# Hybrid retention/MLA step: the sample rows' latents in plain float32 on four column groups, with the first loads reordered

## The chip, the cores and the metric

The kernel runs on one core of a Trainium2 chip. The metric is the device time of one execution in microseconds (us). Before the change the median of 3 runs is 2147.01 us (2147.0 to 2148.47). Verdicts compare medians of runs on the same chip.

## The reference

One layer of a hybrid decoder is computed for 1024 prompt rows and 32 sample rows (8 sequences of 4 tokens), model width 1024. What matters here is its start: the normalised input times one wide matrix, of which the "latent" columns (384 + 256 + 64 = 704) are normalised again and rotated.

```
z = rmsnorm(x, ln_w) @ w_in
rq, rk, rv, rg, cq, ckv, kr, mg, ga, gb = jnp.split(z, ...)
q = (rmsnorm(cq, q_norm_w) @ w_uq).reshape(b, s, MLA_HEADS, MLA_QK)
ckv = rmsnorm(ckv, kv_norm_w)
kr = rope(kr, pos)
```

Behind it come paged attention of the sample rows over 8192 past tokens each, retention, prompt attention, and the output projections. The gates (`rg`, `mg`, `ga`, `gb`) are further columns of `z`.

## The kernel before

All large products take float32 operands split into a high part (rounded to float32r) and a low part (the rest); `mac` issues three matmuls for each product of two such pairs (lines 265 to 267). The high part of a weight is a cast on ACT or POOL, the low part a subtraction on DVE (`lo_of`, L199).

**First stage, the latents.** The 1056 rows are nine tiles: 0 to 7 are the prompt's 128 rows each, tile 8 the 32 sample rows. The order is 0, 1, 8, 2, 3, 4, 5, 6, 7. For each tile:

- `load_x` brings the rows in (L302; four rooms `xt`).
- `turn_tile` squares and sums the rows on ACT (L347, into `xs`), makes the reciprocal root on POOL (`rs_v`, `rs_r`), transposes the tile on PE in eight 128x128 pieces (L322), copies them out of PSUM (L323, `turn`), and stores them (`xTD`).
- `scale_tile` spreads the reciprocal root over the columns with one small matmul on PE (L355), multiplies on DVE (`y`, L358), and makes the high part on ACT (`xh`, L363) and the low part on DVE (`xl`, L364).
- `latent_tile` runs 2 x 8 x 3 = 48 matmuls (columns 0 to 383, then 384 to 703) into PSUM tiles `ac`, of which there are three, then normalises (ACT L398, POOL `rs`, DVE L400), rotates (DVE L374 to L379), stores `la` (two rooms; `latS` for the sample rows) and stores a blockwise transpose (`lt`, L330, `latD`).

The latent weight is 8 blocks of 128 x 704, loaded by `load_lat` into four rooms `wlr`; its high parts are cast alternately on ACT and POOL.

**The filler.** `gate_tiles` gives one column block of 128 gate columns after another: `load_w` loads it in two halves (L245, two rooms `wr`), POOL casts `wh`, DVE makes `wl`, and 72 matmuls follow in three thirds of 352 rows; each third is copied out by ACT (L416, `gev`) and stored (L417, `ga`). `beside` draws such work from the generator `fill` while it runs the first stage, and again beside the sample queries and the paged attention. The sample queries start with transposes of `latS` (L506) and a product of 12 float32 matmuls of 32 rows on four column groups (L527). `page_rows` loads the page table and makes the index column for the gathers; its two tiles share the rooms `xs`.

The written order is not the executed one: a scheduler places the instructions of each engine, and each engine then runs its own list strictly in order. SP issues nearly all loads and stores, also in order.

These lines are the core of the latents' product, and the product by column groups that exists already:

```
for ps, lo, w in ((pq, 0, QL), (pk, QL, KL + ROPE)):
    for k in range(8):
        xk = tuple(v[:, t * P:t * P + n] for v in xn[k])
        wk = tuple(v[:, lo:lo + w] for v in wlat[k])
        mac(ps[:n, :w], xk, wk, k == 0, k == 7)
```

```
pe.matmul(ps[c * NR:(c + 1) * NR, :384], cqT[:, k, :], wq[c][:, k], start=k == 0,
          stop=k == 2, tile_position=(0, c * NR), skip_group_check=True)
```

Of the kernel before, what the change touches and what calls it, by code (L numbers as in the profile page):

```python
# [9 lines left out]
F32 = mybir.dt.float32  # L10
F32R = mybir.dt.float32r
BF16 = mybir.dt.bfloat16
I32 = mybir.dt.int32
# [148 lines left out]
def decode_step(ctx: ExitStack, tc: tile.TileContext, A: dict, O: dict):  # L162
# [20 lines left out]
    def ac():  # L183
        return banks["pool"].tile([P, 512], F32, tag="ac", name="ac", bufs=3)
# [41 lines left out]
    def small(pl, tag, w=1, bufs=4):  # L226
        return pl.tile([P, w], F32, tag=tag, name=tag, bufs=bufs)

    def rstd_of(pl, ss, n, scale, by=pool, w=1):

        v = small(pl, f"rs_v{w}", w, 4 if w == 1 else 2)
        by.tensor_scalar(v[:n], ss[:n], scale, EPS, op0=ALU.mult, op1=ALU.add)
        r = small(pl, f"rs_r{w}", w, 4 if w == 1 else 2)
        pool.tensor_tensor(out=r[:n], in0=v[:n], in1=nhalf[:n].to_broadcast([n, w]), op=ALU.pow)
        return r
# [68 lines left out]

    def load_lat(k):
        hi, lo = (p1.tile([P, NLAT], F32R, tag=f"wl{s}{k}", name=f"wl{s}{k}", bufs=1) for s in "hl")
        raw = p1.tile([P, NLAT], F32, tag="wlr", name="wlr", bufs=4)
        sp.dma_start(raw, w_in[k * P:(k + 1) * P, C_LAT:C_LAT + NLAT])
        (hi_pool if k % 2 else act.copy)(hi, raw)
        lo_of(lo, raw, hi)  # L310
        wlat.append((hi, lo))

    def turn_input(t, src, dst, nf, by=act.copy):

        n = rows(t)
        turned = []
        for half in range(0, nf, 4):
            st = p1.tile([P, 4, P], F32, tag="turn", name="turn", bufs=4)
            w = min(4, nf - half)
            pt = tr()  # L320
            for i in range(w):
                pe.transpose(pt[:, i * P:i * P + n], src[:n, (half + i) * P:(half + i + 1) * P], ident[:n, :n])  # L322
            by(st[:, :w, :n], pt[:, :w * P].rearrange("p (a b) -> p a b", a=w)[:, :, :n])  # L323
# [18 lines left out]
    def turn_tile(t):  # L342
        n = rows(t)
        xt = xts.pop(t)
        ss = small(p1, "ss")
        xs = p1.tile([P, D], F32, tag="xs", name="xs", bufs=2)
        act.activation(xs[:n], xt[:n], AF.Square, accum_out=ss[:n])  # L347
# [35 lines left out]
    latS = lp.tile([NR, NLAT], F32, name="latS")  # L383
    idx = lp.tile([P, NB * NPG // 16], I32, name="idx")

    def latent_tile(t):
        n = rows(t)
        pq, pk = ac(), ac()
        for ps, lo, w in ((pq, 0, QL), (pk, QL, KL + ROPE)):
            for k in range(8):  # L390
                xk = tuple(v[:, t * P:t * P + n] for v in xn[k])
                wk = tuple(v[:, lo:lo + w] for v in wlat[k])
                mac(ps[:n, :w], xk, wk, k == 0, k == 7)
        la = latS if t == 8 else p1.tile([P, NLAT], F32, tag="la", name="la", bufs=2)
        cq, kv, kr = la[:n, 0:QL], la[:n, QL:QL + KL], la[:n, QL + KL:NLAT].unsqueeze(1)
        for src, dst, w, nw in ((pq[:n, :QL], cq, QL, qnw), (pk[:n, :KL], kv, KL, kvw)):
            ss = small(p1, "ss2")
            act.activation(dst, src, AF.Square, accum_out=ss[:n])  # L398
            r = rstd_of(p1, ss, n, 1.0 / w)
            dve.scalar_tensor_tensor(out=dst, in0=src, scalar=r[:n], in1=nw[:n], op0=ALU.mult, op1=ALU.mult)  # L400
        rope_nat(kr, pk[:n, KL:KL + ROPE].unsqueeze(1), t, n, p1, 1, "kro")
        if t < 8:
            sp.dma_start(O["ckv_prompt"][0, 0, t * P:(t + 1) * P, :], kv)
            sp.dma_start(O["krope_prompt"][0, 0, t * P:(t + 1) * P, :], la[:, QL + KL:])
            turn_blocks(latD, p1.tile([P, NLAT], F32, tag="lt", name="lt", bufs=2), la, t, P)
        else:
            sp.dma_start(O["ckv_sample"].rearrange("l b t c -> (l b t) c"), kv)
            sp.dma_start(O["krope_sample"].rearrange("l b t c -> (l b t) c"), la[:n, QL + KL:])

    def gate_tiles(col, dst, fs, func):  # L410
        for f in fs:
            w = load_w(w_in[:, col + f * P:col + (f + 1) * P], 8)

            def evac(j, ps, sl, f=f):
                t = wst.tile([P, TH], F32, tag="gev", name="gev", bufs=2)
                act.activation(t, ps, func)  # L416
                sp.dma_start(dst[f][:, sl], t)  # L417
            yield from gemm(w, xn, evac, 8)
# [6 lines left out]
                 gate_tiles(C_RG, [t[:, f, :] for t in gtD for f in range(4)], range(16), AF.Silu), gate_tiles(C_MG, mgD, range(4), AF.Silu))  # L425

    def page_rows():
        pt_all = p1.tile([P, NB * NPG], I32, tag="xs", name="pt_all", bufs=2)
        sp.dma_start(pt_all, A["page_table"].rearrange("b n -> (b n)").unsqueeze(0).to_broadcast([P, NB * NPG]))
        own = p1.tile([P, NB * NPG], F32, tag="xs", name="own", bufs=2)  # L430
# [5 lines left out]
        dve.tensor_scalar(idx, row, C("mod"), None, op0=ALU.add)  # L436

    head = at["maskT"][0]
# [6 lines left out]
    for k in range(8):  # L445
# [8 lines left out]
    load_x(order[3])  # L454

    def latents():
        for n, t in enumerate(order):
# [5 lines left out]
            if n == 0:  # L463
                turn_tile(order[2])
# [5 lines left out]
            if n == 4:  # L470
                page_rows()
            yield 7.1 if n > 5 else 0.0

    beside(latents(), 3 * 7.1, fill, 36)
# [1151 lines left out]
```

## Time and profile before

| what | value |
|---|---|
| median of 3 runs | 2147.01 us |
| the profiled execution, its own time | 2157.48 us |
| its span, first to last instruction | 2155.6 us |
| PE busy, of the span | 98% |
| DVE / ACT / POOL busy | 58% / 34% / 15% |
| mean granted PE clock | 0.996 |
| mean share of the 16 DMA engines, slice by slice | 0.1 to 0.7, mean 143 GB/s |

The first stage and the filler that stands among it take the first 142 us of the span; after it PE has the paged attention with filler (to about 740 us), retention (to about 1390), prompt attention (to about 1650) and the output projections.

In the timeline a row gives the start and the duration in us, the engine, the line, what is written and read, the shape, the count, and in brackets how long the engine was idle before and what ended that. PE's matmuls overlap: the distance from one start to the next is what a matmul costs, not its duration.

### The profile page before, as it was taken

What the parts mean: (1) busy time and instruction counts of PE and PEld (TensorE: products, weight loads), DVE (VectorE), ACT (ScalarE), POOL (GpSimd) and SP (SyncE); (2) the same over time, 40 slices, a digit from 0 to 9 for tenths busy, and PEclk for the clock granted to TensorE, in tenths of its full rate; (3) what the DMA queues carried; (4) which work ended last, traced back from release to release, by engine and by line L of the source; (5) the groups of instructions that cost most, each with busy time, mean ns of one, the idle gap of its engine ahead of it and who ended that gap; (6) DMA issues with size and microseconds to landing.
All of it is one profiled execution on the core that took longest, in us unless ns stands there. A gap on an engine that the chain in (4) does not pass through costs nothing. (4 is left out here: it accounts for less than half of the span.)

```text
span 2155.6 us, 38512 instructions
## 1 busy us (share of the span) xinstructions
PE 2112.4 (98%) x15192; PEld 1841.9 (85%) x15192; DVE 1260.7 (58%) x2846; ACT 724.1 (34%) x1528; POOL 326.7 (15%) x519
## 2 busy tenths in 40 slices
PE   8999999999999999999999999899999999999998
PEld 7898777777778897888888887788888999999998
DVE  5534555565655346667676774877777353444465
ACT  5412222433433222222222221454556341222243
POOL 2210111111100022222122220122221000000022
PEclk9999999999999999999999999999999999999999
DMA  7476656566565332553634628220112453324243
GB/s 209 123 223 225 238 185 231 200 245 222 186 239 176 112 85 65 162 158 103 217 72 126 198 74 265 69 53 12 38 57 81 143 178 100 95 84 126 79 143 118
DMA packets 325877, 307.84 MB, mean 143 GB/s; under 512 B 91648, under 2 KB 283264, under 8 KB 321600
## 3 DMA queue, kind: packets, MB, share of 16 engines
q1 hardware_dynamic: 316480, 221.50, 34.3%
q0 software_dynamic: 9216, 83.89, 10.3%
q8 instruction: 119, 1.95, 0.4%
q14 instruction: 62, 0.51, 0.1%
HBM read 236.96 MB, written 68.36 MB: 142 GB/s over the span
## 5 line engine op out<-in xcount | busy, mean ns | idle before, releaser
L265 PE MATMUL mm<-xh,wh 128*128 128x352 f32 x1344 | 456.6, 340 | 0.9 <-ACT gev L416 0.8
L267 PE MATMUL mm<-xh,wl 128*128 128x352 f32 x1344 | 435.2, 324 | 2.1 <-DVE wl L199 2.1
L266 PE MATMUL mm<-xl,wh 128*128 128x352 f32 x1344 | 436.1, 324 | 0.0
L265 PEld LDWEIGHTS mm<-xh,wh 128*128 128x128 f32 x1344 | 253.2, 188 | 91.5 <-issue 77.2
L266 PEld LDWEIGHTS mm<-xl,wh 128*128 128x128 f32 x1344 | 254.3, 189 | 3.2 <-issue 1.0
L267 PEld LDWEIGHTS mm<-xh,wl 128*128 128x128 f32 x1344 | 253.9, 189 | 3.3 <-DVE wl L199 2.6
L199 DVE TENSOR_TENSOR wl<-wr,wh 128x512 fp32r<-128x512 f32 (+2 forms) x251 | 172.9, 701 | 121.2 <-ACT wh L246 99.6
L246 ACT CAST wh<-wr 128x512 fp32r<-128x512 f32 x216 | 129.7, 618 | 291.9 <-PE mm L266 215.6
L651 DVE STREAM_TRANSPOSE kt<-craw 128x512 f32<-128x512 f32 x256 | 160.8, 681 | 108.3 <-PE sc L655 73.2
L416 ACT ACTIVATE gev<-mm 128x352 f32<-128x352 f32 x120 | 55.4, 463 | 231.6 <-PE mm L267 149.8
L265 PE MATMUL mm<-mh,wh 128*128 128x352 f32 x384 | 124.6, 325 | 1.4 <-ACT mh L1109 0.8
L266 PE MATMUL mm<-ml,wh 128*128 128x352 f32 x384 | 124.6, 325 | 0.8 <-DVE ml L199 0.6
L267 PE MATMUL mm<-gh,wl 128*128 128x352 f32 x384 | 124.3, 324 | 0.0
L267 PE MATMUL mm<-mh,wl 128*128 128x352 f32 x384 | 124.3, 324 | 0.0
L265 PE MATMUL mm<-gh,wh 128*128 128x352 f32 x384 | 124.2, 324 | 0.0
L266 PE MATMUL mm<-gl,wh 128*128 128x352 f32 x384 | 124.2, 323 | 0.0
L265 PE MATMUL mm<-wv,xh 128*128 128x512 f32 x256 | 103.7, 405 | 0.0
L266 PE MATMUL mm<-wv,xh 128*128 128x512 f32 x256 | 100.9, 394 | 0.0
L267 PE MATMUL mm<-wv,xl 128*128 128x512 f32 x256 | 100.8, 394 | 0.0
L655 PE MATMUL sc<-kt,q 32*32 32x512 f32 x2560 | 92.9, 600 | 0.0
L854 ACT ACTIVATE on<-ac,gb,gs 128x512 f32<-128x512 f32 (+1 forms) x36 | 28.0, 777 | 179.6 <-DVE gb L852 179.6
L1556 POOL TENSOR_TENSOR xr<-x1h,x1l 128x352 f32<-128x352 f32 x24 | 27.1, 1152 | 389.4 <-DVE pT L199 311.3
(383 smaller groups left out, 4537.6 us busy)
## 6 DMA issues: line engine op xcount, KB each, us to landing
wr<-in_w_in_dram SPq DMA_DIRECT2D x144, 256.0 KB, 2.8
st<-in_state_ret_dram SPq DMA_DIRECT2D x32, 512.0 KB, 4.5
out_ret_sample_dram<-st SPq DMA_DIRECT2D x32, 512.0 KB, 3.2
wr<-in_w_ple_gate_dram SPq DMA_DIRECT2D x48, 256.0 KB, 2.9
gt<-gev SPq DMA_DIRECT2D x48, 176.0 KB, 1.9
gl<-go SPq DMA_DIRECT2D x16, 528.0 KB, 5.2
gate<-ga SPq DMA_DIRECT2D x16, 528.0 KB, 3.6
g<-gt SPq DMA_DIRECT2D x32, 256.0 KB, 3.4
```

Of the source, the lines that this page charges most:

```text
L199: dve.tensor_tensor(out=out, in0=src, in1=b32(hi), op=ALU.subtract)
L246: hi_by[0](hi, raw)
L265: pe.matmul(out, wh, xh, start=first, stop=False)
L266: pe.matmul(out, wh, xl, start=False, stop=False)
L267: pe.matmul(out, wl, xh, start=False, stop=last)
L416: act.activation(t, ps, func)
L651: dve.transpose(kt[:, 2 * i + s].rearrange("p (n r) -> p n r", r=32), src)
L655: pe.matmul(sc[32 * v:32 * v + 32, q, :], Q["q4"][qs_, j + v // 2, 2 * (g % 2) + v % 2, :], kt[qs_, v, :], start=n == 0, stop=n == NJ // 2 ...
L854: act.activation(on[:n], po, AF.Identity, bias=nb[:n], scale=s[:n])
L1556: pool.tensor_tensor(out=xr, in0=b32(x1[f][0][:, sl]), in1=b32(x1[f][1][:, sl]), op=ALU.add)
```

## The change

- The sample rows leave the split: `sample_latents` multiplies the raw float32 weight `wlr` with `xS` (the transposed sample rows times `ln_w`, made on POOL) in 32 plain float32 matmuls. Each gives 176 of the 704 columns in its own group of 32 array columns; for each of the eight weight blocks there are four. They are issued inside tile 0's product. The reciprocal root (`r8`) is multiplied in afterwards, when `latent_tile(8)` copies the four groups out (ACT) into a tile `las` and scales it (DVE). The 48 matmuls of tile 8 go. `scale_tile(8)` stays, since the filler needs these rows.
- The raw weight must now stay until its sample matmuls have read it; its rooms go from four to five. `xs` goes from two rooms to one, `la` from two to three (`las` takes one).
- The sample rows are loaded and turned before tile 1, the second weight block and those behind it are loaded later.
- The page table's two tiles use the rooms `wr` of the weight loads, and its load is issued at the third tile of the order, the arithmetic at the fifth.
- `gate_tiles` yields once after its load, and `next(fill)` at the sixth tile issues the first gate weight's load there.

```diff
-        raw = p1.tile([P, NLAT], F32, tag="wlr", name="wlr", bufs=4)
+        raw = p1.tile([P, NLAT], F32, tag="wlr", name="wlr", bufs=5)
...
-        wlat.append((hi, lo))
+        wlat.append((hi, lo, raw))
...
-        xs = p1.tile([P, D], F32, tag="xs", name="xs", bufs=2)
+        xs = p1.tile([P, D], F32, tag="xs", name="xs", bufs=1)
...
+        if t == 8:
+            r8 = small(p1, "r8", 1, 1)
+            pool.tensor_copy(r8[:n], r[:n])
+            r = r8
...
+    NG = NLAT // 4
+
+    def sample_latents(k):
+        for r in range(4):
+            pe.matmul(few[0][r * NR:(r + 1) * NR, :NG], few[1][:, k], wlat[k][2][:, r * NG:(r + 1) * NG], start=k == 0, stop=k == 7,
+                      tile_position=(0, r * NR), skip_group_check=True)
...
+        if t < 8:
+            pq, pk = ac(), ac()
+            for ps, lo, w in ((pq, 0, QL), (pk, QL, KL + ROPE)):
+                for k in range(8):
...
+                    mac(ps[:n, :w], xk, wk, k == 0, k == 7)
+                    if t == 0 and lo == 0:
+                        sample_latents(k)
+        else:
+            raw = p1.tile([NR, NLAT], F32, tag="la", name="las", bufs=3)
+            for r in range(4):
+                act.activation(raw[:, r * NG:(r + 1) * NG], few[0][r * NR:(r + 1) * NR, :NG], AF.Copy)
+            dve.tensor_scalar(raw, raw, few[2][:NR], None, op0=ALU.mult)
+            pq, pk = raw[:, :QL], raw[:, QL:]
+        la = latS if t == 8 else p1.tile([P, NLAT], F32, tag="la", name="la", bufs=3)
...
             w = load_w(w_in[:, col + f * P:col + (f + 1) * P], 8)
+            yield 0.0
...
-        pt_all = p1.tile([P, NB * NPG], I32, tag="xs", name="pt_all", bufs=2)
+        pt_all = wst.tile([P, NB * NPG], I32, tag="wr", name="pt_all", bufs=2)
...
+    load_x(8)
     turn_tile(0)
     scale_tile(0)
     order = [0, 1, 8, 2, 3, 4, 5, 6, 7]
-    for k in range(8):
+    load_lat(0)
+    load_x(1)
+    turn_tile(8)
+    few = [mm(), wst.tile([P, 8, NR], F32, tag="gev", name="xS", bufs=2), turned[8][0]]
+    for half, st in enumerate(turned[8][1]):
+        fs = slice(4 * half, 4 * half + 4)
+        pool.tensor_tensor(out=few[1][:, fs], in0=st[:, :, :NR], in1=lnw[:, fs].unsqueeze(2).to_broadcast([P, 4, NR]), op=ALU.mult)
+    for k in range(1, 8):
         load_lat(k)
-        if k % 4 == 0:
-            load_x(order[1 + k // 4])
...
+            if n in (2, 4):
+                next(table)
+            if n == 5:
+                next(fill)
```

The executed order, where the prediction needs it. First PE at the start of tile 0's product, before: transposes of tile 0 and tile 1 with their scales, then latent matmuls of tile 0 (`xh_112` is the first of eight blocks of the high part).

```order
L322 MATMUL tr<-cst,xt 128x128 x8
L355 MATMUL tr<-cst,rs_r_247 128x128
L265 MATMUL ac<-wlh_187,xh_112 128x384
L266 MATMUL ac<-wll_188,xh_112 128x384
L265 MATMUL ac<-wlh_187,xh_112 128x320
L266 MATMUL ac<-wll_188,xh_112 128x320
L267 MATMUL ac<-wlh_187,xl_113 128x384
```

The same place now (`mm<-wlr,xS` is a sample matmul, x4 one weight block):

```order
L394 MATMUL mm<-wlr,xS 32x176 x4
L265 MATMUL ac<-wlh_226,xh_114 128x384
L265 MATMUL ac<-wlh_226,xh_114 128x320
L394 MATMUL mm<-wlr,xS 32x176 x4
L265 MATMUL ac<-wlh_189,xh_112 128x384
L266 MATMUL ac<-wll_190,xh_112 128x384
L394 MATMUL mm<-wlr,xS 32x176
L266 MATMUL ac<-wll_227,xh_114 128x384
L267 MATMUL ac<-wlh_226,xl_115 128x384
L265 MATMUL ac<-wlh_232,xh_116 128x384
L394 MATMUL mm<-wlr,xS 32x176 x3
```

The 32 sample matmuls stand in nine groups (4, 4, 4, 1, 3, 1, 7, 1, 7) among tile 0's matmuls; only two of tile 1's matmuls are left there, where before there were ten.

Second, POOL around the first gate weight's cast (`wh<-wr`). Before, it stood between the roots of tiles 5 to 7:

```order
L234 TENSOR_TENSOR rs_r_1017<-rs_v_1015,cst 128x1
L196 TENSOR_SCALAR wh<-wr 128x512
L232 TENSOR_SCALAR rs_v_1061<-ss 128x1
L232 TENSOR_SCALAR rs_v_1134<-ss_1132 128x1
L234 TENSOR_TENSOR rs_r_1063<-rs_v_1061,cst 128x1
```

Now (`ss_1530` and `ss_1537` are the sums of tile 7's two parts):

```order
L232 TENSOR_SCALAR rs_v_1532<-ss_1530 128x1
L234 TENSOR_TENSOR rs_r_1534<-rs_v_1532,cst 128x1
L232 TENSOR_SCALAR rs_v_1539<-ss_1537 128x1
L234 TENSOR_TENSOR rs_r_1541<-rs_v_1539,cst 128x1
L196 TENSOR_SCALAR wh<-wr 128x512 x6
```

The cast has moved behind the last root of the last latent tile. On DVE the first `wl` likewise stands behind tile 7's rotation and one blockwise transpose now:

```order
L420 SCALAR_TENSOR_TENSOR la<-ac,rs_r_1541,kvw 128x256
L378 TENSOR_TENSOR kro_1544<-ac,ropeM 128x32
L379 TENSOR_TENSOR kro_1545<-ac,ropeM 128x32
L380 TENSOR_TENSOR la<-kro_1544,kro_1545 128x32
L381 TENSOR_TENSOR kro_1544<-ac,ropeM 128x32
L382 TENSOR_TENSOR kro_1545<-ac,ropeM 128x32
L383 TENSOR_TENSOR la<-kro_1544,kro_1545 128x32
L330 STREAM_TRANSPOSE lt<-la 128x704
L199 TENSOR_TENSOR wl<-wr,wh 128x512 x2
```

On PE all latent matmuls now come first, then the transposes of `latS`, then 288 filler matmuls (four gate blocks) in a row, then the 12 matmuls of the sample queries in one group; before, the filler stood in pieces among tiles 6 and 7, and the 12 in three groups. From there on, the lists of all engines are the same as before.

Third, SP's list where gate weights are loaded (`wr`) and thirds stored (`ga_74` to `ga_76` are the first three gate blocks). Before:

```order
L417 DMA ga_74<-gev 128x352 x2
L245 DMA wr<-in_w_in_dram 128x4x128 x2
L417 DMA ga_74<-gev 128x352
L403 DMA out_ckv_prompt_dram<-la 128x256
L404 DMA out_krope_prompt_dram<-la 128x64
L245 DMA wr<-in_w_in_dram 128x4x128
L332 DMA latD<-lt 32x22x32 x4
L417 DMA ga_75<-gev 128x352 x2
```

Now:

```order
L438 DMA ga_74<-gev 128x352 x2
L245 DMA wr<-in_w_in_dram 128x4x128 x2
L423 DMA out_ckv_prompt_dram<-la 128x256
L424 DMA out_krope_prompt_dram<-la 128x64
L332 DMA latD<-lt 32x22x32
L438 DMA ga_74<-gev 128x352
L332 DMA latD<-lt 32x22x32 x3
L438 DMA ga_75<-gev 128x352 x2
L245 DMA wr<-in_w_in_dram 128x4x128 x2
```

Before, half of the next block's weight was already asked for ahead of `ga_75`; now each block's weight stands behind the second third of the block ahead of it.

More of the change, by code (lines that the diff above doesn't have):

```diff
@@ L384, in decode_step @@
     idx = lp.tile([P, NB * NPG // 16], I32, name="idx")
+    NG = NLAT // 4
[3 more added lines that the diff above has]
+                      tile_position=(0, r * NR), skip_group_check=True)
     def latent_tile(t):
         n = rows(t)
[L388 to L394 removed]
+        if t < 8:
+            pq, pk = ac(), ac()
+            for ps, lo, w in ((pq, 0, QL), (pk, QL, KL + ROPE)):
+                for k in range(8):
+                    xk = tuple(v[:, t * P:t * P + n] for v in xn[k])
+                    wk = tuple(v[:, lo:lo + w] for v in wlat[k][:2])
+                    mac(ps[:n, :w], xk, wk, k == 0, k == 7)
[8 more added lines that the diff above has]
+        la = latS if t == 8 else p1.tile([P, NLAT], F32, tag="la", name="la", bufs=3)
         cq, kv, kr = la[:n, 0:QL], la[:n, QL:QL + KL], la[:n, QL + KL:NLAT].unsqueeze(1)
@@ L427, in page_rows @@
     def page_rows():
-        pt_all = p1.tile([P, NB * NPG], I32, tag="xs", name="pt_all", bufs=2)
+        pt_all = wst.tile([P, NB * NPG], I32, tag="wr", name="pt_all", bufs=2)
         sp.dma_start(pt_all, A["page_table"].rearrange("b n -> (b n)").unsqueeze(0).to_broadcast([P, NB * NPG]))
-        own = p1.tile([P, NB * NPG], F32, tag="xs", name="own", bufs=2)
+        yield
+        own = wst.tile([P, NB * NPG], F32, tag="wr", name="own", bufs=2)
         dve.tensor_copy(own, pt_all)
@@ L456, in latents @@
     def latents():
+        table = page_rows()
         for n, t in enumerate(order):
```

6 lines of the change are left out of this document (1 added, 5 removed).

## Prediction

> **What bounds the kernel now.** First the page's head and the list of waits, PE alone, for the first 170 us.
>
> ```profile
> span 2155.6 us, 38512 instructions
> PE 2112.4 (98%) x15192; PEld 1841.9 (85%) x15192; DVE 1260.7 (58%) x2846; ACT 724.1 (34%) x1528; POOL 326.7 (15%) x519
> ...
> PE tr L355 <- POOL rs_r L234: 7.1, 4, 3.3
> PE mm L267 <- DVE wl L199: 2.1, 2, 1.5
> ```
>
> PE is busy for 98% of the span, so only what PE does or waits for in the first stage can pay; a third of its 43 us of idling lies there. The largest waits are scales (L355) that lack a reciprocal root and a first gate weight (L267) that lacks its low part. The timeline of PE shows where:
>
> ```profile
> 12.57 0.67 PE L265 MATMUL ac<-wlh,xh 128*128 128x384 f32 x1
> ...
> 14.21 0.52 PE L265 MATMUL ac<-wlh,xh 128*128 128x384 f32 x1
> 14.53 0.52 PE L266 MATMUL ac<-wll,xh 128*128 128x384 f32 x1
> ...
> 27.66 0.40 PE L355 MATMUL tr<-cst,rs_r 32*128 32x32 f32 x2 [1.91 <-POOL rs_r L234]
> ...
> 36.50 0.42 PE L265 MATMUL ac<-wlh,xh 128*32 128x384 f32 x1
> ...
> 44.13 0.31 PE L267 MATMUL ac<-wlh,xl 128*32 128x320 f32 x1
> ...
> 44.41 0.42 PE L265 MATMUL ac<-wlh,xh 128*128 128x384 f32 x1
> ...
> 45.20 1.03 PE L322 MATMUL tr<-cst,xt 128*128 128x128 f32 x8
> 45.99 0.42 PE L266 MATMUL ac<-wll,xh 128*128 128x384 f32 x1
> ...
> 78.48 0.49 PE L355 MATMUL tr<-cst,rs_r 128*128 128x128 f32 x2 [3.28 <-POOL rs_r L234]
> ...
> 90.56 0.43 PE L267 MATMUL mm<-xh,wl 128*128 128x352 f32 x1 [1.46 <-DVE wl L199]
> ...
> 108.66 0.43 PE L267 MATMUL mm<-xh,wl 128*128 128x352 f32 x1 [0.61 <-DVE wl L199]
> ```
>
> Tile 8's 48 matmuls start at 36.50 and end with the one at 44.13: 7.8 us, as much as a tile of 128 rows. Tile 2 begins at 44.41. Eight transposes take 0.8 (45.20 to 45.99). The first matmuls come at a slow clock: 0.32 from start to start (14.21 to 14.53) where 384 columns take 0.175 later. From 44.41 on PE waits 3.28 + 1.46 + 0.61 = 5.35 us.
>
> I make the sum in two pieces, from the start to tile 2, and from tile 2 to the end of L527. Behind that the lists of all engines are as before, so what is won by then should stay.
>
> **Up to tile 2.** Removed: 7.8 us of tile 8. Added: 32 sample matmuls. The only rows of this kind among other matmuls are those of L527 (also float32, 32 rows, four column groups; two records make one instruction):
>
> ```profile
> 150.64 0.32 PE L266 MATMUL mm<-xl,wh 128*128 128x352 f32 x1
> 150.89 0.83 PE L527 MATMUL mm<-early 128*32 128x384 f32 x2
> 151.66 0.43 PE L267 MATMUL mm<-xh,wl 128*128 128x352 f32 x1
> 151.92 0.32 PE L265 MATMUL mm<-xh,wh 128*128 128x352 f32 x1
> ...
> 153.38 0.32 PE L265 MATMUL mm<-xh,wh 128*128 128x352 f32 x1
> 153.63 2.12 PE L527 MATMUL mm<-early 128*32 128x384 f32 x18
> 155.68 0.43 PE L266 MATMUL mm<-xl,wh 128*128 128x352 f32 x1
> ```
>
> A matmul of 352 columns occupies 0.16, so one L527 instruction takes 151.66 - 150.80 = 0.86 and lengthens the next step from 0.16 to 0.26: 0.96. Nine take 155.68 - 153.54 = 2.14. So each further one costs (2.14 - 0.86) / 8 = 0.16, four at once stream 384 columns in 0.64, and 0.32 is paid per group for going in and out. For 176 columns I scale the stream: 0.29 for the first, 0.07 for each further one, and keep the 0.32: a group of n costs 0.54 + 0.07 n. Nine groups with 32 come to 7.1 us, almost the 7.8 that go. The bounds: if 0.32 weren't paid and only the stream counted, 32 x 0.07 = 2.3; if a group cost what it costs at 384 columns, 9 x 0.96 + 23 x 0.16 = 12.3. I take 7.1, since the nearest rows differ only in width.
>
> The Trainium skill, "TensorEngine Tiling (Array Packing)", Key Properties, says that changing the tiling mode drains the TensorE; by that the nine groups pay eighteen changes, and the sum is the 7.1 above. "TensorE: Matmul & The Clock Gate" of the Trainium skill, Measured speedup vs the span model, has tiles overlap at about 4 ns each and names no such price; by it alone the sum would be nearer 2.3. The 0.96 for a lone instruction speaks for the drain.
>
> When does PE begin? The sample rows are turned ahead of tile 1, and the first sample group (four, at the slow clock, about 1.3) and tile 1's transposes stand ahead of tile 0's first matmul. In return `xh` of tile 0 no longer waits behind tile 1's sum of squares on ACT. Both move it by about 1 us; I leave it at 12.6, within 1 either way. From there, in PE's order: tiles 0 and 1 at 7.75 each, 15.5; six matmuls at the slow clock, +1.0; 28 sample matmuls in eight groups, 8 x 0.54 + 28 x 0.07 = 6.3; two scales 0.6; tile 2's transposes with their switch, 0.9. Tile 1 ends at 12.6 + 24.3 = 36.9. The wait of 1.91 for tile 8's scale, with the slow clock after it, goes: the scale comes early. The weights' later issue I cost at nothing, because PE's own work has become the longer chain there; if a load lands 2 us late behind the sample rows' stores on SP, that is 2 us.
>
> Next is tile 2's own chain. Before, tile 8's 7.8 us stood between tile 2's scale and its first matmul. Now only tile 3's transposes do, and ACT has other work first:
>
> ```profile
> 35.69 0.38 ACT L398 ACTIVATE la<-ac 128x256 f32<-128x256 f32 x1 [1.38 <-PE ac L267]
> ...
> 36.87 2.45 ACT L363 ACTIVATE xh<-y,lnw 128x128 fp32r<-128x128 f32 x8
> 39.22 0.57 ACT L323 COPY turn<-tr 128x512 f32<-128x512 f32 x1
> ...
> 41.01 0.48 ACT L398 ACTIVATE latS<-ac 32x384 f32<-32x384 f32 x1 [1.22 <-PE ac L267]
> ...
> 44.91 1.04 ACT L347 ACTIVATE xs<-xt 128x1024 f32<-128x1024 f32 x1
> ```
>
> In ACT's new list tile 1's second sum (0.38 and about 0.2 for its read-out, 0.2 after PE's end), the sample's first sum (0.48 + 0.2) and a copy (0.57) precede `xh` (0.3 each). That is 2.4 us from tile 1's last matmul to tile 2's first, and 0.3 of waits for `xl` follow: tile 2 effectively starts at 39.6 in place of 44.4. **Won: 4.8 us.**
>
> **From tile 2 to the end of L527.** Removed: the 5.35 us of waits. The page table no longer takes tile 6's room `xs`, and the first gate weight is loaded 40 us ahead. L527's three pieces become one: before, 1.18 for the first piece (two instructions) + 0.96 + 2.25 = 4.4; now 0.96 + 11 x 0.16 = 2.7; 1.7 won. Together 7.0.
>
> Three waits come in. (a) Behind the last latent tile the first gate block needs its cast, which POOL now has behind that tile's root. Rows from PE, ACT, POOL and DVE for that tile before:
>
> ```profile
> 128.09 0.31 PE L267 MATMUL ac<-wlh,xl 128*128 128x320 f32 x1
> ...
> 128.50 0.39 ACT L398 ACTIVATE la<-ac 128x256 f32<-128x256 f32 x1 [2.95 <-PE ac L267]
> ...
> 126.54 0.62 POOL L196 TENSOR_SCALAR wh<-wr 128x512 fp32r<-128x512 f32 x1
> ...
> 129.33 0.55 POOL L234 TENSOR_TENSOR rs_r<-rs_v,cst 128x1 f32<-128x1 f32 x1
> ...
> 127.20 0.69 DVE L199 TENSOR_TENSOR wl<-wr,wh 128x512 fp32r<-128x512 f32 x1
> 129.91 0.48 DVE L400 SCALAR_TENSOR_TENSOR la<-ac,rs_r,kvw 128x256 f32<-128x256 f32 x1 [2.02 <-POOL rs_r L234]
> ...
> 131.40 0.91 DVE L330 STREAM_TRANSPOSE lt<-la 128x704 f32<-128x704 f32 x1
> ```
>
> Counted from the last latent matmul's start (128.09): root done 129.88, `wh` 130.5. DVE runs the rotation to 131.40, the transpose to 132.3, then `wl` to 132.9, which is 4.85 later. PE has only 1.0 of work ready ahead of that L267 (0.15 step, transposes of `latS` 0.5, two filler matmuls). Wait: 3.85. Below, were DVE to take `wl` first, it would be 1.9; nothing shows more than 4.5.
>
> (b) Filler now stands alone for four blocks. The next block's weight is asked for only behind the second third's store, and before, latents covered most of this:
>
> ```profile
> 116.13 0.46 ACT L416 ACTIVATE gev<-mm 128x352 f32<-128x352 f32 x1 [3.10 <-PE mm L267]
> 120.01 0.47 ACT L416 ACTIVATE gev<-mm 128x352 f32<-128x352 f32 x1 [3.42 <-PE mm L267]
> ...
> 117.05 1.00 SPq L245 DMA_DIRECT2D wr<-in_w_in_dram  x2
> ...
> 120.08 0.62 POOL L196 TENSOR_SCALAR wh<-wr 128x512 fp32r<-128x512 f32 x1 [7.71 <-DMA wr<-in_w_in_dram]
> ...
> 120.73 0.69 DVE L199 TENSOR_TENSOR wl<-wr,wh 128x512 fp32r<-128x512 f32 x1 [7.64 <-POOL wh L196]
> ```
>
> From the second third's copy (116.13) to `wh` ready is 120.70 - 116.13 = 4.6, to `wl` 5.3. PE's third third takes 120.01 - 116.13 = 3.9, and it is free 0.3 before that copy starts. So it waits 1.0 for `wh` and 0.3 for `wl`: 1.3 at each of three boundaries, 3.9. Below it is 0 where a latent is left to fill in, above 2 each with a slower landing.
>
> (c) Tile 6's scale follows tile 5's last filler-free stretch: its sum of squares (1.04) stands on ACT behind all eight `xh` of tile 5 (2.45), which stand behind tile 4's first sum; by these rows the root is about 1 us late (0 to 2).
>
> Sum: 7.0 - 3.85 - 3.9 - 1.0 = -1.75. **Whole change: 4.8 - 1.75 = 3.0 us won.** The profiled execution took 2157.48, 10.5 more than the median, mostly outside what is touched; I take the difference over unchanged: 2147.0 - 3.0 = 2144.0.
>
> **Rivals.** (1) No price per group: the sample matmuls cost 28 x 0.07 = 2.0 in place of 6.3 in that stretch: 4.3 more won, 2139.7, if weights land in time. The lone 0.96 speaks against it. (2) The new waits (a) to (c) don't come, because filler covers them or the pieces are quicker: 8.75 more, 2135.3. The waits that go support it in kind, PE's order speaks against it. (3) Slower: the clock. If PE stays at half clock while it is fed in small groups, each further us at half clock costs 0.5 us. Before, it was slow from 12.57 to about 15.4. I count it to 14.6; from 20.6 on the gain of 3.0 is gone, and to the end of tile 0's product at 28.4 it costs 6.9: 2150.9. For it: PE ran 0.32 steps after 1.91 us of idling at 27.66. Against: it was fed in pieces before too, and was fast by 16.
>
> "TensorE: Matmul & The Clock Gate" of the Trainium skill, What's actually happening, has the clock follow activity in free-running windows of about 3.4 us; by it wait (a) may add a slow window, an estimated 1.7 us.
>
> **How the numbers follow.** My sum 0.50, (1) 0.22, (2) 0.14, (3) 0.14. A measurement of this kernel tells about 0.2% from no change, 4.3 us: 2142.7 and 2151.3. (1) and (2) are faster by more than that: 0.36. My sum is within. Of (3), 0.04 is within, and with a slow window at (a) or a late load 0.10 is beyond: same 0.54, slower 0.10. Likeliest 2144.0. The range leaves out part of (2) and of the slow end: 2136.5 to 2151.5. The first matmul's place, the price of a group and (a) to (c) span it.
>
> **What would show it.** Nine L394 groups with steps of 0.6 to 1.1; tile 2's first matmul near 39.6; no wait of 3 us at tile 6's scale; a wait near 4 us at the first L267 `mm`, behind the `latS` transposes; three near 1.3 at later blocks. Wrong would be: tile 2 before 36 (groups cheaper), the first gate block without a wait, or 0.32 steps beyond 20 us.

## The result and the profile after

| | kernel before | changed kernel |
|---|---|---|
| median | 2147.01 us (2144.41 to 2148.68, 7 runs) | 2157.63 us (2152.98 to 2163.7, 7 runs) |
| ratio, with its 95% interval | 1 | 1.0049 (1.0038 to 1.006) |
| the profiled execution | 2157.48 us | 2155.49 us |

The changed kernel is 10.6 us slower where 3.0 us faster was forecast, outside the range. The two profiles don't show it: the one of before had taken 10.5 us more than its median. So a second profile of the kernel before was taken (`before_again`, 2147.92 us), and the pages are read against that one.

Page of the changed kernel:

```profile
span 2153.7 us, 38535 instructions
PE 2108.8 (98%) x15208; PEld 1839.2 (85%) x15208; DVE 1258.9 (58%) x2847; ACT 725.0 (34%) x1532; POOL 327.4 (15%) x522
```

What PE waits for between 30 and 174 us in the changed kernel (total, times, longest):

```profile
PE mm L265 <- POOL wh L196: 7.7, 4, 3.9
PE tr L359 <- POOL rs_r L234: 2.2, 2, 1.2
PE mm L267 <- DVE wl L199: 2.0, 1, 2.0
PE mm L265 <- ACT gev L437: 1.3, 1, 1.3
PE tr L575 <- DVE early L576: 0.7, 1, 0.7
```

The waits for scales have shrunk, as meant. In their place the filler (L265, L267 `mm`) waits for its weights. Where, the timeline of PE in the changed kernel shows:

```profile
11.89 0.94 PE L265 MATMUL ac<-wlh,xh 128*128 128x384 f32 x2
...
19.03 0.34 PE L265 MATMUL ac<-wlh,xh 128*128 128x384 f32 x1
19.30 0.49 PE L394 MATMUL mm<-wlr,xS 128*32 128x176 f32 x2
19.71 0.45 PE L266 MATMUL ac<-wll,xh 128*128 128x384 f32 x1
20.00 0.34 PE L267 MATMUL ac<-wlh,xl 128*128 128x384 f32 x1
...
23.05 0.34 PE L265 MATMUL ac<-wlh,xh 128*128 128x384 f32 x1
23.32 0.80 PE L394 MATMUL mm<-wlr,xS 128*32 128x176 f32 x14
24.05 0.41 PE L267 MATMUL ac<-wlh,xl 128*128 128x320 f32 x1
24.30 0.33 PE L266 MATMUL ac<-wll,xh 128*128 128x384 f32 x1
...
38.28 0.42 PE L265 MATMUL ac<-wlh,xh 128*128 128x384 f32 x1
...
65.69 0.49 PE L359 MATMUL tr<-cst,rs_r 128*128 128x128 f32 x2 [1.04 <-POOL rs_r L234]
...
92.40 0.43 PE L265 MATMUL mm<-xh,wh 128*128 128x352 f32 x1 [1.61 <-POOL wh L196]
95.04 0.66 PE L267 MATMUL mm<-xh,wl 128*128 128x352 f32 x1 [2.01 <-DVE wl L199]
109.86 0.43 PE L265 MATMUL mm<-xh,wh 128*128 128x352 f32 x1 [1.17 <-POOL wh L196]
122.81 0.43 PE L265 MATMUL mm<-xh,wh 128*128 128x352 f32 x1 [0.95 <-POOL wh L196]
138.74 0.66 PE L265 MATMUL mm<-xh,wh 128*128 128x352 f32 x1 [3.93 <-POOL wh L196]
...
152.95 2.14 PE L557 MATMUL mm<-early 128*32 128x384 f32 x24
...
165.61 0.43 PE L265 MATMUL mm<-xh,wh 128*128 128x352 f32 x1 [1.33 <-ACT gev L437]
...
173.36 1.87 PE L582 MATMUL mm<-early 128*128 128x32 f32 x16
```

Tile 2 starts at 38.28 where it had started at 44.41. From there the four gate blocks wait at each of their starts. The last row is the place used from here on: **M**, the first product over the heads (`mm<-early`, 128x32, x16). Ahead of M every kernel of this study has run the same 360 filler matmuls; only tile 8's work differs (32 sample matmuls or 48 of the split), and the 30 that one run adds. M stands at 173.36 here; in the first profile of before at 167.76, in the second at 167.02:

```profile
167.02 1.87 PE L552 MATMUL mm<-early 128*128 128x32 f32 x16
```

So the changed kernel is 6.3 us behind at M. At the end of the span it is 7.7 us behind (2153.7 and 2146.0).

The windows of the changed kernel, PE alone (width, busy and count, granted clock, DMA share, GB/s):

```profile
92.80:99.60 6.80, 4.79 (x17) 0.50 0.00 0
137.20:144.00 6.80, 5.26 (x18) 0.50 1.07 388
167.90:171.30 3.40, 3.40 (x15) 0.50 0.40 140
```

Behind the waits the granted clock is a half, twice for 6.8 us and once for 3.4 us. At half clock work takes twice its time (below, 13 matmuls start in 4 us where 27 do at full clock), so half of the busy time in these windows is lost: (4.79 + 5.26 + 3.40) / 2 = 6.7 us. In `before_again` the clock of these stretches is 1.00.

The first profile of before was long in a stretch that the change doesn't touch: in the paged attention, from the first `x<-craw,pT` product behind M (at 218.31) to the last (at 725.39), it took 507.1 us, `before_again` 499.1 and the changed kernel 498.9.

### The profile page after: what moved, and what is told of

It is laid out like the page before. It is cut to its first block, busy times and chain, and to the rows that moved or that the text cites. A ratio compares the mean times of both kernels' runs of the same rounds, so it can differ in the third digit from the quotient of the medians.

```text
span 2153.7 us, 38535 instructions
## 1 busy us (share of the span) xinstructions
PE 2108.8 (98%) x15208; PEld 1839.2 (85%) x15208; DVE 1258.9 (58%) x2847; ACT 725.0 (34%) x1532; POOL 327.4 (15%) x522
## 4 chain that ended last, share of the span: by engine, by line
PE 87%; DMA 3%; DVE 3%; issue 3%; ACT 2%; POOL 2%; SPq 0%; DVEq 0%; ACTq 0%; POOLq 0%
PE mm L265 21%; PE mm L266 20%; PE mm L267 20%; PE sc L685 4%; PE x L716 3%; PE ac L266 2%; PE ac L265 2%; PE ac L267 2%; PE mm L1343 2%; DMA wr<-in_w_in_dram 1%; PE tr L1329 1%; PE ac L1286 1%; PE tr L895 1%; PE x L710 1%; DMA st<-in_state_ret_dram 1%
## 5 line engine op out<-in xcount | busy, mean ns | idle before, releaser
L265 PE MATMUL mm<-xh,wh 128*128 128x352 f32 x1344 | 458.2, 341 | 10.2 <-POOL wh L196 7.7
L267 PE MATMUL mm<-xh,wl 128*128 128x352 f32 x1344 | 436.3, 325 | 2.0 <-DVE wl L199 2.0
L265 PEld LDWEIGHTS mm<-xh,wh 128*128 128x128 f32 x1344 | 254.3, 189 | 101.7 <-issue 77.9
L267 PEld LDWEIGHTS mm<-xh,wl 128*128 128x128 f32 x1344 | 254.9, 190 | 2.7 <-DVE wl L199 2.3
L265 PE MATMUL mm<-mh,wh 128*128 128x352 f32 x384 | 124.6, 325 | 1.4 <-ACT mh L1139 0.8
L267 PE MATMUL mm<-mh,wl 128*128 128x352 f32 x384 | 124.3, 324 | 0.0
L267 PE MATMUL mm<-gh,wl 128*128 128x352 f32 x384 | 124.3, 324 | 0.0
L265 PE MATMUL mm<-gh,wh 128*128 128x352 f32 x384 | 124.2, 324 | 0.0
L265 PE MATMUL mm<-wv,xh 128*128 128x512 f32 x256 | 103.7, 405 | 0.0
L267 PE MATMUL mm<-wv,xl 128*128 128x512 f32 x256 | 100.7, 394 | 0.0
```

The lines of the kernel that those rows point to most:

```text
L265: pe.matmul(out, wh, xh, start=first, stop=False)
L267: pe.matmul(out, wl, xh, start=False, stop=last)
```

## The experiments

All kernels were timed against the kernel before on their own chip. M is from one profile each.

| kernel | median, us | ratio (95% interval) | M, us |
|---|---|---|---|
| changed kernel | 2157.63 | 1.0049 (1.0038 to 1.006) | 173.36 |
| before_again | 2146.78 | 0.9999 (0.999 to 1.0008) | 167.02 |
| latents_only | 2146.65 | 1.0001 (0.9992 to 1.001) | 162.37 |
| page_only | 2146.16 | 0.9998 (0.9989 to 1.0007) | 165.91 |
| fill_at_3 | 2153.29 | 1.0032 (1.002 to 1.0045) | 167.79 |
| no_early_weight | 2147.72 | 1.0003 (0.9993 to 1.0012) | 161.66 |
| second_weight_ahead | 2154.67 | 1.0044 (1.0031 to 1.0058) | 170.07 |
| reorder_only | 2150.12 | 1.0019 (1.001 to 1.0028) | 170.14 |
| two_weights_early | 2145.77 | 0.9994 (0.9985 to 1.0003) | 158.94 |
| two_weights_earlier | 2146.17 | 1.0 (0.9991 to 1.0009) | 159.00 |
| wait_filled | 2147.22 | 0.9998 (0.9989 to 1.0007) | 160.07 |
| two_early_no_samples | 2143.49 | 0.9982 (0.9973 to 0.9991) | 163.62 |
| on a chip where the kernel before takes 2154.2: | | | |
| two_early_no_samples_2 | 2151.74 | 0.9988 (0.998 to 0.9997) | 163.70 |
| early_rows_no_samples | 2152.46 | 0.9993 (0.9985 to 1.0002) | 164.56 |
| rooms_only | 2153.81 | 0.9999 (0.9989 to 1.0009) | 164.84 |
| early_rows_two_weights | 2151.84 | 0.9991 (0.9982 to 1.0) | 163.54 |

### Where the loss arises, and which part brings it

**before_again** is the kernel before, unchanged.

> The unchanged kernel, for a second profiled execution of it: the first took 2157.48, 10.5 over the median, and its part up to the end of L527 (155.68) is only 0.65 longer than that of the changed kernel (155.02). Theory A (the loss of the change arises in the first stage): here L527 ends about 10 us sooner than in the first profile, at 144 to 148, and what follows takes about 2000 as in both profiles. Theory B (the loss arises behind the first stage, where all lists are the same): L527 ends near 155 again and what follows takes about 1990. Ratio to the kernel before 0.999 to 1.001 either way.

Neither theory had the place right: the end of L527 came only 0.74 us sooner (155.68 and 154.94), and 8.0 of the other 8.9 us of the first profile were in the paged attention. But the end of L527 is not the place to compare at, since 16 filler matmuls fewer stand ahead of it in the changed kernel (288 and 304). At M the changed kernel is behind by 6.3 of the 7.7 us that the spans differ by: theory A.

**latents_only**: the sample latents without the rest.

```
 xs: bufs=1 -> 2     la: bufs=3 -> 2     pt_all, own: tag "wr" -> "xs"
-            if n in (2, 4):
-                next(table)
+            if n == 4:
+                next(table)
+                next(table)
-            yield 0.0
-            if n == 5:
-                next(fill)
```

> The sample latents alone: the page table back in xs with two rooms, its work in one piece, no early gate weight, two rooms la. PE's order has the gate blocks among tiles 5 to 7 again, as in the kernel before. Theory A1 (the filler that stands uncovered behind the latents costs the time, by its waits of 3.6, 1.2, 1.0 and 3.9 and by the half clock behind them, 6.8 us at half speed twice): faster than the kernel before by the 6.1 us that the start won, 2141. Theory A2 (the sample matmuls on column groups cost more than the start shows): 2155 or more.

The loss is gone, so it isn't the sample matmuls (A2 falls). M is 4.65 us ahead of before, near the 6.1, but the time is that of the kernel before. This comes up again below.

**page_only**: the kernel before with the page table in `wr`, its load at the third tile and its arithmetic at the fifth as in the change.

```
-        xs = ..., tag="xs", name="xs", bufs=2)
+        xs = ..., tag="xs", name="xs", bufs=1)
-        pt_all = p1.tile(..., tag="xs", ...)
+        pt_all = wst.tile(..., tag="wr", ...)
...
```

> The kernel before with only the page table moved into the rooms wr (one room xs), nothing else. By PE's order this alone puts the four gate blocks in a row behind the latents. Theory A1: the waits and half clock of the uncovered filler come here too, without the 6.1 us of the start; the wait of 3.3 at tile 6's scale goes: slower than before by 8 to 17 us, 2155 to 2164. Theory A2: 2142 to 2147, since only the wait goes and no column groups are added.

A1 falls too. The four blocks stand in a row here as in the changed kernel, and the first one waits (2.13 and 2.10), but the other three don't wait, and nothing is slower. So it isn't the missing cover by itself. The difference from the changed kernel stands on SP. The changed kernel:

```profile
101.45 4.23 SPq L438 DMA_DIRECT2D ga<-gev  x2
105.77 1.00 SPq L245 DMA_DIRECT2D wr<-in_w_in_dram  x2
...
127.93 3.91 SPq L438 DMA_DIRECT2D ga<-gev  x2
131.94 1.04 SPq L245 DMA_DIRECT2D wr<-in_w_in_dram  x2
133.15 0.47 SPq L545 DMA_DIRECT2D early<-in_w_uq_dram  x1
```

and page_only:

```profile
98.90 0.98 SPq L245 DMA_DIRECT2D wr<-in_w_in_dram  x2
99.94 1.05 SPq L332 DMA_DIRECT2D latD<-lt  x2
105.68 0.34 SPq L417 DMA_DIRECT2D ga<-gev  x1
...
110.03 1.01 SPq L245 DMA_DIRECT2D wr<-in_w_in_dram  x2
```

In page_only the second block's weight is asked for at 98.90, ahead of the first block's stores, and the third at 110.03, still within the first block. In the changed kernel the second weight comes only behind two of these stores (105.77), and all later ones a block later than in page_only: the fourth is asked for at 131.94, when 3 us of the third block are left, and just ahead of the sample queries' weights (`early`). How long these loads take in the changed kernel, from issue to landing:

```profile
DMA to landing us min/median/max: 3.0/3.4/6.3
```

The longest belong to the fourth weight: asked for at 131.94, it is cast from 138.07 on. POOL in the changed kernel:

```profile
138.07 1.82 POOL L196 TENSOR_SCALAR wh<-wr 128x512 fp32r<-128x512 f32 x2 [6.38 <-DMA wr<-in_w_in_dram]
```

PE's wait there is the 3.93.

The late request alone doesn't cost the time either. The kernel before has it too. SP in its first profile:

```profile
94.89 3.91 SPq L417 DMA_DIRECT2D ga<-gev  x2
98.91 1.01 SPq L245 DMA_DIRECT2D wr<-in_w_in_dram  x2
```

Its second weight also stands behind two stores of the first block, but PE had latent matmuls until 107.1, and its block waited 0.61. The waits come where a late request and uncovered blocks meet.

**fill_at_3**, the early weight two tiles sooner:

```
-            if n == 5:
+            if n == 3:
                 next(fill)
```

> The changed kernel with the first gate weight asked for two tiles sooner (n == 3 in place of 5): the first gate block then stands among tile 5's and 6's work and only three blocks stand behind the latents. Theory A1: the waits of 1.6 and 2.0 at the first block and the 6.8 us of half clock behind them go, 3.6 + 3.4 = 7 us off the changed kernel, about 2150.5. Theory A2 or B: within 2 us of the changed kernel, 2156 to 2159.

5.6 us of the loss go by M, 4.3 by the medians. The first block is covered now; the wait (1.62 and 2.10) has moved to the second block, and one of 3.26 remains at the fourth.

**no_early_weight**: the changed kernel without `yield 0.0` and `next(fill)`.

```
             w = load_w(...)
-            yield 0.0
-            if n == 5:
-                next(fill)
```

> The changed kernel without the early first gate weight: no next(fill), no yield behind the load; sample latents, page table in wr and rooms as changed. PE's list is word for word that of the changed kernel; on SP the second block's weight stands ahead of the first stores again, as in page_only. The place to look at is the first product over the heads (M: 167.02 in before_again, 173.36 in the changed kernel, 165.91 in page_only), ahead of which all kernels have done the same work. Theory A3 (the early request moves the second weight behind two stores, each later weight comes a third of a block late, and PE waits and drops to half clock): the waits of 1.17, 0.95, 3.93, 1.33, 0.66 and the half clock behind them (2.6 + 1.7) go, M at 160 to 163; time 2141 to 2147. Theory A4 (it is the uncovered filler together with the sample latents, whatever SP does): M at 171 to 174, 2154 to 2158.

SP in no_early_weight:

```profile
96.12 0.98 SPq L245 DMA_DIRECT2D wr<-in_w_in_dram  x2
...
102.31 0.34 SPq L437 DMA_DIRECT2D ga<-gev  x1
```

This settles which part brings the loss (theory A3). PE has the same work, in the same order but for a few matmuls at the starts of blocks (so not quite word for word), the second weight is asked for ahead of the first store again, and 10 us go by the medians, 11.7 by M (161.66, 2147.72 us). No block but the first waits for its weight.

**reorder_only**: page_only with the early weight, without the sample latents.

```
             w = load_w(...)
+            yield 0.0
+            if n == 5:
+                next(fill)
```

> The kernel before with the page table in wr (as page_only) and the early first gate weight, without the sample latents. Theory A3: against page_only (M 165.91, no change of time) the weights come late, as in the changed kernel: M at 174 to 179, slower than the kernel before by 8 to 13 us. Theory A4 (the early weight matters only together with the sample latents, or not at all): M 165 to 168, within 3 us of the kernel before.

Slower than before by 0.19%, page_only isn't: the early weight costs here too, 4.2 us by M and 3.3 by the medians of its chip (2146.79 before), where 8 to 13 were expected. Less, since here the first block's weight was cast between tile 7's roots and the first block didn't wait.

**second_weight_ahead** asks for the second block's weight ahead of the first block's matmuls, in the changed kernel:

```
             yield 0.0
+            if col == C_GA and f < 1:
+                ahead.append(load_w(w_in[:, col + (f + 1) * P:...], 8))
```

> The changed kernel with the early first gate weight, and the second block's weight asked for in the program ahead of the first block's matmuls: on SP it moves from behind two stores of the first block to ahead of them; the third weight still stands behind two stores of the second. Theory A3: the wait of 1.17 at the second block goes; the third and later weights come as late as before, so 0.95 to 1.2 and 3.9 stay: M 171 to 172.5, 2153 to 2157. If the lateness is carried from the first boundary alone: M 163, 2147. Theory A4: M 173, no difference.

M is 3.3 us better: the second block's wait is gone, those of the third (0.76) and the fourth (2.44) remain. So the lateness is not carried from one boundary, each weight has its own.

**two_weights_early** asks for the first two weights at the fifth and sixth tile, and for the third and fourth ahead of the matmuls of the block before:

```
             yield 0.0
+            if col == C_GA and f < 3:
+                ahead.append(load_w(w_in[:, col + (f + 1) * P:...], 8))
+                yield 0.0
-            if n == 5:
+            if n in (4, 5):
                 next(fill)
```

> The changed kernel with the first gate weight asked for at the fifth tile and the second at the sixth, and the weights of blocks 3 and 4 ahead of the matmuls of blocks 2 and 3. Both first weights are cast on POOL and DVE ahead of tile 7's roots and rotation, the first block stands inside tile 7. Theory A3: no wait of 1.6 + 2.0 behind the latents and no half clock there (6 off), and no waits at the block boundaries (8.6 off): M at 158 to 161, time 2140 to 2146, faster than both kernels if nothing behind gives it back. Theory A4: M not below 170.

No block waits for its weight, M is 14.4 us ahead of the changed kernel and 8.1 ahead of before. The early weight is harmless once the second one is early too. The median is 11.9 us below the changed kernel, but not surely below before. **two_weights_earlier**, the same with `if n in (3, 4)`, gives no more:

> As two_weights_early, but the two gate weights are asked for one and two tiles sooner (fourth and fifth tile), so that the first block stands between tiles 5 and 6 and the second among tile 6. If covering the filler further wins: M 155 to 158, 2142 to 2145. If nothing is left to cover (two_weights_early has no wait over 1.4 behind tile 2's scale): M 158 to 160, 2144 to 2147, the same as the kernel before.

### The half clock

**wait_filled** is no_early_weight with 30 added matmuls, whose result nobody reads, in the place of the first block's waits (2.15 and 2.33 us there):

```
+        junk = tr()
+        for _ in range(30):
+            pe.matmul(junk[:, :TH], xn[0][0][:, :P], xn[1][0][:, :TH], start=True, stop=True)
```

> The kernel no_early_weight with 30 added matmuls of 352 columns on PE behind the transposes of latS, whose result nobody reads; they take about 30 x 0.15 = 4.5 us, as long as the two waits that stand there (2.15 and 2.33 in no_early_weight). All else is word for word that kernel. Theory C1 (PE drops to half clock because it stood idle there, 6.8 us at half speed from 93.4 on, of which 4 fall on work): the first gate block starts at the same place, the clock stays full, M 159.3 to 160.5 in place of 161.66, time 1 to 3 us below no_early_weight. Theory C2 (the half clock comes with the work of that place or at random): half clock at 93 to 100 as before, M 161.5 to 162.5, and no gain.

PE from 96 to 100 us, first no_early_weight:

```profile
96.00:100.00 4.00, 3.85 (x13) 0.50 0.79 180
```

and wait_filled:

```profile
96.00:100.00 4.00, 4.00 (x27) 1.00 0.81 183
```

With PE kept busy the clock stays full, and 27 matmuls start in place of 13. M is 1.6 us better, as C1 has it: the half clock comes from standing idle there. One profile could be chance, but the others agree: all seven profiles with a pair of waits of 1.6 to 2.8 us at their first uncovered block show 0.50 behind it. The median hardly moves (2147.72 and 2147.22), so what is won at M is given back later here too.

### What the sample latents are worth

**two_early_no_samples** is two_weights_early without the sample latents: tile 8's 48 matmuls are in the split again, its rows are loaded and turned as in the kernel before, and the rooms of the raw weight and of `la` are those of before too.

```
-        if t < 8:
             pq, pk = ac(), ac()
...
-                    if t == 0 and lo == 0:
-                        sample_latents(k)
```

> The kernel two_weights_early without the sample latents: the kernel before with the page table in wr, both first gate weights early, and weights 3 and 4 ahead; tile 8 is again 48 matmuls. It tells what the sample latents are worth by themselves where the filler is covered. By the start alone (tile 2 at 44.41 and 38.28) M should be 158.94 + 6 = 165. If that gain reaches the end: slower than two_weights_early by 4 to 6 us, 2149 to 2152. If it is given back behind the first stage (waits on transfers and half clock there): 2145 to 2148 with M at 165.

M is 4.7 us later than with the sample latents (6 were computed), yet the median is 2.3 us *lower* (ratios 0.9994 and 0.9982, whose intervals overlap): the gain at M doesn't reach the end. The two waits behind M in which some of it goes stand near 880 and 1320 us. The timeline of ACT and PE, and the list of PE's waits from 650 to 1400 us, in two_weights_early:

```profile
876.24 0.62 ACT L246 CAST wh<-wr 128x512 fp32r<-128x512 f32 x1 [1.34 <-DMA wr<-in_w_in_dram]
...
876.91 0.43 PE L265 MATMUL mm<-xh,wh 128*128 128x352 f32 x1 [1.09 <-ACT wh L246]
```

```profile
PE ac L1072 <- DMA st<-in_state_ret_dram: 2.1, 1, 2.1
```

and in two_early_no_samples:

```profile
879.65 0.62 ACT L246 CAST wh<-wr 128x512 fp32r<-128x512 f32 x1 [0.19 <-DMA wr<-in_w_in_dram]
```

```profile
PE ac L1048 <- DMA st<-in_state_ret_dram: 1.1, 2, 0.7
```

Between 800 and 1400 us all eight kernels with sample latents wait 0.9 to 1.9 us for such casts and 1.6 to 2.5 for the retention state. The kernels without them, five profiles up to here, wait 0 to 0.2 and 0.9 to 1.1. The next four runs ask which piece of the edit does that.

**two_early_no_samples_2**, the same kernel again:

> two_early_no_samples once more, for its interval (0.9982, 0.9973 to 0.9991) and a second profile. If its gain is real: 0.997 to 0.999, M near 163.6, and near 880 us no wait of PE for a weight cast of about 1 us. If it was chance: 0.999 to 1.001.

Below the kernel before again, by 0.12%.

**early_rows_no_samples**: the rooms, the early sample rows and the order of first loads as in the change, but tile 8 in the split and, as in no_early_weight, no early weight:

```
-                    if t == 0 and lo == 0:
-                        sample_latents(k)
-        else:
-            raw = p1.tile([NR, NLAT], F32, tag="la", name="las", bufs=3)
...
```

> no_early_weight without the sample matmuls: the sample rows are still loaded and turned ahead of tile 1, the rooms are those of the change, but tile 8 is again 48 matmuls in the split. In all eight kernels with sample latents PE waits 0.9 to 1.9 near 880 us for a weight cast on ACT and 1.6 to 2.5 for the retention state; in the five without, 0 to 0.2 and 0.9 to 1.1. Theory D1 (the later loss comes with the rooms or the order of the first loads): the wait near 880 is here too, 1 us or more. Theory D2 (it comes with the sample matmuls themselves): 0 to 0.2. M 162 to 166 by either; time 2143 to 2147 by D2.

No wait for the cast, 1.2 for the state. **rooms_only**, page_only with the rooms of the change:

```
-        raw = ..., name="wlr", bufs=4)
+        raw = ..., name="wlr", bufs=5)
-        la = ..., name="la", bufs=2)
+        la = ..., name="la", bufs=3)
```

> page_only with the rooms of the change (five for the raw weight, three for la), nothing else. D1 with the rooms: a wait of 1 us or more near 880. D1 with the order of loads, or D2: 0 to 0.2 as in page_only.

No wait for the cast, 0.8 for the state. So the later waits come with the sample matmuls and what they bring (D2), not with rooms or load order. These four runs share one chip, on which no kernel with the sample latents was run. How 32 matmuls at 20 us delay a load at 876 us stays open: nothing in these profiles links the two.

**early_rows_two_weights**, the edit of two_weights_early made in early_rows_no_samples:

> early_rows_no_samples with the two gate weights early, as in two_weights_early: all of the change's reordering, mended, without the sample latents. The early sample rows take the wait of 1.9 at tile 8's scale away. If reordering alone wins: M 160 to 163 and 2141 to 2145, faster than the kernel before. If the loss near 880 and 1320 comes with the early rows: 2145 to 2147.

0.9991 (0.9982 to 1.0), with 0.2 and 1.2 us of waits at the two places: no better than two_early_no_samples, which is the one version here whose interval lay below the kernel before, and it did so on two chips.

## Why the prediction was wrong, by its own steps

**Up to tile 2: right, a little small.** 4.8 was forecast, 44.41 - 38.28 = 6.1 came (5.4 against `before_again`, where tile 2 starts at 43.66). The price of a group held: around the single instruction at 19.30 two matmuls of 0.175 took 20.00 - 19.03 = 0.97, so it cost 0.62 (forecast 0.61); the group of seven at 23.32 cost 24.30 - 23.05 - 0.32 = 0.93 (1.03). The first latent matmul came at 11.89 in place of 12.6. Rival 1 (no price per group) is out. That a change of the tiling mode drains TensorE, as the Trainium skill has it in "TensorEngine Tiling (Array Packing)", Key Properties, agrees with the 0.62. No run separates the change of mode from the change to plain float32 that comes with it.

**Waits that go: right.** The 3.28, 1.46 and 0.61 are gone, and L527 runs in one piece (155.02 - 152.95 = 2.1, where 2.7 was forecast and 4.4 had been).

**New waits (a) and (c): right.** (a) 3.85 was forecast, 1.61 + 2.01 = 3.62 came; (c) 1.0 and 1.04. Rival 2 is out.

**The step that failed most: the half clock, left out of the sum.** The sum priced each new wait at its length alone. The text placed the slow clock at the start (rival 3), where the steps of 0.32 were over by 13.8, and at (a) only in a sentence beside the sum, an estimated 1.7. It came behind (a), behind the fourth block's wait and behind the last two waits ahead of M, and cost 2.4 + 2.6 + 1.7 = 6.7 us. "TensorE: Matmul & The Clock Gate" of the Trainium skill, "HAM oscillation — how this bites in real kernels", has PE drop its clock after an idle stretch longer than a window of about 3.4 us. The 3.93 agrees. The waits of 1.61 and 2.01 at (a), and of 1.33 and 0.66, are each shorter, and the half clock followed them too; here the measurement decides.

**New waits (b): mis-sized, and only half explained.** Three times 1.3 was forecast, from one load that landed in a quiet place: 3.9. They came as 1.17, 0.95 and 3.93: 6.05. The fourth load, beside the sample queries' weights, takes 6 us to land in place of 3.4. That latents covered the late requests before is so (the rows at 94.89). But the requests didn't have to be late: page_only and no_early_weight have the same uncovered row of blocks and none of these waits. The early first weight, which the text credited as a gain ("the first gate weight is loaded 40 us ahead"), is what keeps every later weight behind two stores. The 40 us is wrong too: the load is asked for at 75.41, 17 us ahead of its use, and only 13.4 us sooner than in no_early_weight (88.79).

**An end too early.** The sum stopped at L527. Behind it stand the waits of 1.33 and 0.66, and 16 filler matmuls that the kernel before runs ahead of L527's end. PE's order is therefore not the same from L527 on; both kernels have run the same filler again only at M.

The terms up to M, against the first profile (plus is slower, in us; the text rounds its -3.1 to 3.0 won):

| term | forecast | came |
|---|---|---|
| up to tile 2 | -4.8 | -6.1 |
| waits that go | -5.35 | -5.35 |
| L527 in one piece | -1.7 | -2.3 |
| (a) | +3.85 | +3.6 |
| (b) | +3.9 | +6.05 |
| (c) | +1.0 | +1.0 |
| waits behind L527 | none | +2.0 |
| half clock | none | +6.7 |
| sum | -3.1 | +5.6 |

M itself moved by 173.36 - 167.76 = +5.60.

**"What is won by then should stay": wrong.** 6.3 us of loss at M became 7.7 in the profiles and 10.6 in the medians. As far as is recorded, the clock doesn't account for it. Over 7 executions of the changed kernel its mean is 0.9950, over 82 of the kernel before (those beside the first eleven experiments) 0.9967; the 0.0017 is worth 3.6 us, less than the 6.7 lost ahead of M. In the profiles it is the kernel before that loses clock behind M: `before_again` reads 0.98 from 690 to 800 and from 1280 to 1380 us, the changed kernel 1.00 in both. Gains were given back in other kernels as well: two_weights_early is 8.1 ahead at M and 1.0 by its median (2146.79 before on its chip). The waits near 880 and 1320 are part of it (1.2 + 1.6 us in the changed kernel, 0.2 + 1.1 in `before_again`); the rest stays open.

That the first profile's excess lay outside what is touched held (paged attention). The last four runs' chip took 505.0 to 507.4 us for the stretch that took 507.1 in that profile, all other profiles 498.7 to 500.2; so the first profile was probably of such a chip, and the times beside it were not. That wasn't tried.

## What to carry to other kernels

An earlier load can make later loads late: when a prefetch is moved, follow in the issuing queue where the *next* loads of the same rooms land, and count each load's lead over its use in blocks. Price a wait on TensorE together with the half clock that may stand behind it; where it came in the changed kernel it cost another 0.66 to 0.85 of the waits. Compare two profiles at a place ahead of which both have done the same work, and only profiles whose untouched stretches agree.

## What the runs showed of the hardware that was not expected

- Not every wait brings the half clock. A wait of 3.29 us at tile 6's scale was followed by it in latents_only (granted clock 0.50 from 74.4 to 77.6) and one of 3.27 in before_again was not:

```profile
74.40:77.60 3.20, 3.20 (x14) 0.50 0.41 123
```

```profile
78.00:82.00 4.00, 4.00 (x31) 1.00 0.32 93
```

  Even one and the same kernel differs: in the first profile of before the granted clock is 0.50 from 29.4 to 32.6, behind the wait of 1.91 for tile 8's scale, and in `before_again` it stays 1.00 behind the same wait (1.90). The same wait can thus cost 1.6 us more or nothing more.
- At the start of the changed kernel matmuls of 384 columns step by 0.32 us (12.62 to 12.94), nearly twice their later 0.175, while the granted clock reads 1.00 from 12 to 14 us.
- The same stretch of the paged attention took 498.7 to 500.2 us in twelve profiles, and 505.0 to 507.4 in five, four of them from one chip.
